# Token shift on two engines, softmax division after the value products, fused gate factors: one change to a two-layer encoder trunk

## The chip, the cores and the metric

The kernel runs on one core of one Trainium2 chip. The metric is the device time of one execution in microseconds, from several runs of the same kernel. Beside the runs there is one profiled execution, whose trace gives the start and length of each instruction on each engine: TensorE (PE, with its weight loads PEld), VectorE (DVE), ScalarE (ACT), GpSimd (POOL) and SyncE (SP), which issues most of the DMAs.

## What is computed

The input is 1024 frames of 1024 channels in float32. Layer 0 has an input projection whose columns feed two mixers: an RWKV-7 recurrence with 8 heads of 64, and a chunked band attention with 8 heads of 64. Layer 1 is a convolution module. Each layer ends with a squared-ReLU MLP. The change touches the two mixers of layer 0:

```python
# RWKV-7 group
p = p + (token_shift(p) - p) * mu                  # p[t-1] and p[t] mixed
r, k, v, xw, xa, xg = jnp.split(p, split_at, axis=-1)
w = -softplus(-(w0 + tanh(xw) @ w2)) - 0.5
decay = exp(-exp(w))
a = sigmoid(a0 + xa @ a2)
kk = normalise(k * k_k)                            # per head
k = k * (1 + (a - 1) * k_a)
# per step: S = S * decay + (S @ -kk) (kk * a)^T + v k^T ;  y = S @ r

# band attention, a chunk of 64 frames sees itself and 8 chunks before it
s = q @ k^T * HEAD_DIM ** -0.5 + bias
probs = jax.nn.softmax(s, axis=-1)
o = probs @ v
```

## The kernel before

Activations lie with channels on the 128 partitions and frames along the free dimension; the 1024 frames are done as two halves of 512. A dense matrix product (`gemm`, line 216) holds 128 output channels of 512 frames in one PSUM bank `d` and splits both operands into a rounded and a remaining part, so that each product is three matmuls, lines 263 to 265. The weights come by DMA (`wr`, line 203) and are split by ScalarE (`wh`, L207) and VectorE (`wl`, L208). The input projection's value columns are done with the operands the other way round and 256 columns at a time (L362 to L364); they are its last part in each half.

The recurrence (`rwkv`, line 375) takes blocks of 256 frames and pairs of heads, eight units in each half. Each unit has three stages. `prep` loads a tile `pt` of 257 frames from DRAM and mixes each frame with the one before (`mix`, L422 and L423, 14 times in a block of four units), makes decay and gate (L487 to L499, `ta` being the gate's tanh), the normalised key and the tiles `ar` and `bk` (L511 to L530), and their gram products (L549). The result goes out to DRAM and comes back in another layout (`msc`, `nb`). `stage2` inverts a triangular matrix on VectorE (L575 to L587), stores and loads the inverse through DRAM (`xsc`, `xdt`) and completes it with small matmuls (L612 and L622). `stage3` runs the chain over the chunks (L665, L670, L677, then L687 and L691) and the output norm (L700 to L718), and stores to `yd`.

The attention (`attention`, line 737) takes a head pair and 128 queries at a time, 32 groups in all. It makes scores in a PSUM bank `a`, of which there are two (L795, L797), adds the bias and finds the maximum (L799), takes the exponential with its sum (L806), divides (L807, L808), transposes the probabilities on TensorE (L817), copies them out (L818), multiplies by the values into another bank `a` (`ob`, L824), copies that out (`yo`, L827) and stores to `yd`.

The order of the instructions on each engine is set when the program is built. The code gives each piece a level: weight loads and evacuations come first, then the recurrence, then the attention, and the dense matmuls last, so that those fill what the mixers leave open on TensorE. On the chip each engine then takes its instructions strictly in that order. The dense work beside the first half's mixers is the input projection of both halves; beside the second half's mixers it is the output projection (`mixer_out`, which loads `yd` as `mh`) and the MLP of the first half. After the mixers there is only dense work and the convolution.

## Time and profile before

| | |
|---|---|
| runs, median (lowest to highest) | 2561.08 us (2558.75 to 2570.02) |
| profiled execution | 2570.09 us |
| its span, first to last instruction | 2568.2 us |
| granted TensorE clock, mean | 0.978 |
| TensorE busy | 2480.4 us, 97% |
| VectorE busy | 1848.3 us, 72% |
| ScalarE busy | 1143.9 us, 45% |
| instructions | 37380 |

Busy time is the union of an engine's instructions. A matmul's record is longer than the time it adds, since matmuls overlap. The granted clock is the share of full speed that TensorE had.

### The profile page before, as it was taken

To read this page: it belongs to the slowest core of one execution; us is meant where nothing else is said; L and a number is where in the kernel's file an instruction comes from. 1 tells how busy PE (TensorE), PEld (TensorE's weight loads), DVE (VectorE), ACT (ScalarE), POOL (GpSimd) and SP (SyncE) were. 2 spreads that over 40 slices of the span, in tenths; PEclk is the share of its full clock that TensorE was granted. 3 is DMA by queue.
4 is the path that set the end of the run, shared out by engine and by line. 5 is a ranking of instruction groups with operands and counts; after the bars stand their busy time and mean duration, and the time that the engine had idled before them with its cause. 6 is when DMAs were issued, how large, how long until landed. Compare 5 with 4: busy or idle time off the path is not lost.

```text
span 2568.2 us, 37380 instructions
## 1 busy us (share of the span) xinstructions
PE 2480.4 (97%) x12892; PEld 1971.0 (77%) x12892; DVE 1848.3 (72%) x3948; ACT 1143.9 (45%) x2224; POOL 111.6 (4%) x285
## 2 busy tenths in 40 slices
PE   8888999989999999999999999999999999999998
PEld 6667666757676767788888888888888888888887
DVE  5677788658788888546999974679999465544444
ACT  5345545555556655444343333533423355423324
POOL 1011001110000000000100000000000000000000
PEclk9898999989899999999999999999999999999999
DMA  8544444444333332236333333433333335333332
GB/s 266 157 141 137 115 121 119 140 130 119 95 104 107 102 101 81 77 107 197 95 93 100 96 99 99 140 115 95 95 99 99 99 91 156 95 95 98 99 97 68
DMA packets 476462, 291.24 MB, mean 113 GB/s; under 512 B 40416, under 2 KB 453472, under 8 KB 476272
## 3 DMA queue, kind: packets, MB, share of 16 engines
q1 hardware_dynamic: 466080, 258.11, 35.1%
q0 software_dynamic: 9152, 29.36, 3.3%
q8 instruction: 102, 1.67, 0.3%
q10 hardware_dynamic: 1040, 1.38, 0.2%
q14 instruction: 88, 0.72, 0.1%
HBM read 254.12 MB, written 37.77 MB: 114 GB/s over the span
## 4 chain that ended last, share of the span: by engine, by line
PE 82%; DVE 7%; DMA 6%; issue 3%; ACT 1%; SPq 0%; POOL 0%; ACTq 0%; DVEq 0%; POOLq 0%
PE d L264 23%; PE d L263 23%; PE d L265 23%; DMA nb<-msc 3%; DVE wl L208 1%; PE w L549 1%; PE a L824 1%; DVE pr L584 1%; DMA wr<-in_w_in_dram 1%; PE a L817 1%; PE c L665 1%; PE a L795 1%; DVE xi L587 1%; PE c L670 1%; DMA pt<-pd 1%
## 5 line engine op out<-in xcount | busy, mean ns | idle before, releaser
L207 ACT CAST wh<-wr 128x512 fp32r<-128x512 f32 x744 | 460.7, 621 | 988.9 <-PE d L264 897.2
L263 PE MATMUL d<-xh,wh 128*128 128x512 f32 x1872 | 748.4, 400 | 6.1 <-ACT xh L153 4.2
L264 PE MATMUL d<-xl,wh 128*128 128x512 f32 x1872 | 746.6, 399 | 0.8 <-DVE xl L154 0.4
L265 PE MATMUL d<-xh,wl 128*128 128x512 f32 x1872 | 746.3, 399 | 0.9 <-DVE wl L208 0.9
L208 DVE TENSOR_TENSOR wl<-wr,wh 128x512 fp32r<-128x512 f32 x744 | 501.9, 685 | 190.0 <-ACT wh L207 135.0
L263 PEld LDWEIGHTS d<-xh,wh 128*128 128x128 f32 x1872 | 356.9, 191 | 81.2 <-ACT xh L153 4.7
L264 PEld LDWEIGHTS d<-xl,wh 128*128 128x128 f32 x1872 | 356.5, 190 | 74.8 <-DVE xl L157 1.3
L265 PEld LDWEIGHTS d<-xh,wl 128*128 128x128 f32 x1872 | 356.5, 190 | 74.6 <-DVE wl L208 1.6
L263 PE MATMUL d<-mh,wh 128*128 128x512 f32 (+1 forms) x1040 | 405.9, 390 | 0.0
L264 PE MATMUL d<-ml,wh 128*128 128x512 f32 (+1 forms) x1040 | 405.2, 390 | 0.0
L265 PE MATMUL d<-mh,wl 128*128 128x512 f32 (+1 forms) x1040 | 404.9, 389 | 0.0
L947 DVE SCALAR_TENSOR_TENSOR cv<-u,dwt,cv 128x512 f32<-128x512 f32 x480 | 332.4, 746 | 0.7
L264 PEld LDWEIGHTS d<-ml,wh 128*128 128x128 f32 x1040 | 195.7, 188 | 38.9
L265 PEld LDWEIGHTS d<-mh,wl 128*128 128x128 f32 x1040 | 195.5, 188 | 39.1
L263 PEld LDWEIGHTS d<-mh,wh 128*128 128x128 f32 x1040 | 195.6, 188 | 38.4 <-issue 0.2
L846 DVE TENSOR_TENSOR x<-d,x 128x512 f32<-128x512 f32 (+1 forms) x146 | 97.6, 680 | 142.5 <-PE d L265 142.2
L888 DVE SCALAR_TENSOR_TENSOR t<-d,rstd 128x512 f32<-128x512 f32 x128 | 86.3, 686 | 101.2 <-PE d L265 98.1
L584 DVE TENSOR_TENSOR pr<-nb,xi 128x16 f32<-128x16 f32 (+15 forms) x256 | 101.0, 395 | 2.6
L894 DVE TENSOR_TENSOR ml<-t,mh 128x512 fp32r<-128x512 f32 x128 | 87.8, 688 | 13.5 <-ACT mh L892 10.9
L890 ACT ACTIVATE t<-t 128x512 f32<-128x512 f32 x128 | 80.1, 626 | 18.9 <-DVE t L888 18.4
L892 ACT ACTIVATE mh<-t 128x512 fp32r<-128x512 f32 x128 | 78.9, 616 | 0.0
L587 DVE TENSOR_REDUCE xi<-pr 128x8 f32<-128x16 f32 (+15 forms) x256 | 73.9, 289 | 2.4
(261 smaller groups left out, 2452.5 us busy)
## 6 DMA issues: line engine op xcount, KB each, us to landing
wr<-in_up_dram SPq DMA_DIRECT2D x256, 256.0 KB
wr<-in_dn_dram SPq DMA_DIRECT2D x256, 256.0 KB
wr<-in_w_in_dram SPq DMA_DIRECT2D x104, 256.0 KB
wr<-in_pw_dram SPq DMA_DIRECT2D x96, 256.0 KB
nb<-msc SPq DMA_DIRECT2D x16, 512.0 KB
wr<-in_w_out_dram SPq DMA_DIRECT2D x32, 256.0 KB
pd<-t POOLq DMA_DIRECT2D x28, 256.0 KB, 3.0
x<-xd SPq DMA_DIRECT2D x24, 256.0 KB
```

The costliest lines, as they stand in the source:

```text
L207: nc.scalar.copy(hi[:], raw[:])
L208: nc.vector.tensor_tensor(out=lo[:], in0=raw[:], in1=hi[:].bitcast(F32), op=ALU.subtract)
L263: nc.tensor.matmul(q[:, cols], hi, xh[:, cols], start=(k == 0), stop=False)
L264: nc.tensor.matmul(q[:, cols], hi, xl[:, cols], start=False, stop=False)
L265: nc.tensor.matmul(q[:, cols], lo, xh[:, cols], start=False, stop=(k == KT - 1))
L584: nc.vector.tensor_tensor(out=pr[:, :, :, 0:n], in0=pairs[:, r, :, 0:n].unsqueeze(2).to_broadcast([P, 2, 4, n]), in1=xi[:, :, 0:n].unsquee ...
L587: nc.vector.tensor_reduce(out=xi[:, :, n - 2 : n].rearrange("p j r -> p r j"), in_=pr[:, :, :, 0:n], op=ALU.add, axis=AX.X)
L846: nc.vector.tensor_tensor(out=xs[m][:, cols], in0=q[:, cols], in1=xs[m][:, cols], op=ALU.add)
L888: nc.vector.scalar_tensor_tensor(out=t[:], in0=q[:], scalar=0.0, in1=rstd[:], op0=ALU.max, op1=ALU.mult)
L890: nc.scalar.activation(sq[:], t[:], AF.Square)
L894: nc.vector.tensor_tensor(out=lo[:], in0=sq[:], in1=hi[:].bitcast(F32), op=ALU.subtract)
L947: nc.vector.scalar_tensor_tensor(out=c[:], in0=u[:, tap : tap + T], scalar=dw(tap), in1=c[:], op0=ALU.mult, op1=ALU.add)
```

## The change

The vector of coefficients gets 14 more columns, one minus `mu`. `mix` no longer takes a difference on VectorE: ScalarE scales the current frame by one minus `mu`, and VectorE adds the frame before times `mu`. The gate's tanh moves up beside the decay's. The gate's factor (tanh + 1) / 2 is no tile of its own: VectorE adds 1 and multiplies by the inverse decay in one instruction, and the factor 0.5 goes into the next one. In the attention the probabilities are not divided. The two heads' reciprocals of the sums go into a small tile `rr`; after the value products two more matmuls per group spread them over 64 partitions each (weights: one column of `rr`, repeated; moving operand: the identity), into the same PSUM bank. ScalarE copies them to `yo`, and VectorE multiplies the value products by them on the way out.

```diff
+    OMM = VOFF["dw"]
+    nc.vector.tensor_scalar(vec[:, OMM : OMM + 14], vec[:, 0:14], -1.0, 1.0, op0=ALU.mult, op1=ALU.add)
...
-            nc.vector.tensor_tensor(out=d[:], in0=t[:, 0:RT], in1=t[:, 1 : RT + 1], op=ALU.subtract)
-            nc.vector.scalar_tensor_tensor(out=dst, in0=d[:], scalar=v("mu", ct), in1=t[:, 1 : RT + 1],
+            nc.scalar.activation(d[:], t[:, 1 : RT + 1], AF.Copy, scale=vec[:, OMM + ct : OMM + ct + 1])
+            nc.vector.scalar_tensor_tensor(out=dst, in0=t[:, 0:RT], scalar=v("mu", ct), in1=d[:],
                                            op0=ALU.mult, op1=ALU.add)
...
             nc.scalar.activation(tw[:], wps, AF.Tanh, bias=half[:, hp : hp + 1], scale=0.5)
+            ta = e()
+            nc.scalar.activation(ta[:], aps, AF.Tanh, bias=half[:, 4 + hp : 5 + hp], scale=0.5)
             nc.scalar.activation(wx[:, :, 1 : C + 1], d3(tw[:]), AF.Exp, bias=kc[:, 3:4], scale=c1)
...
             yield
-            ta = e()
-            nc.scalar.activation(ta[:], aps, AF.Tanh, bias=half[:, 4 + hp : 5 + hp], scale=0.5)
             ksq = e()
...
-            nc.vector.tensor_scalar(aa[:], ta[:], 0.5, 0.5, op0=ALU.mult, op1=ALU.add)
-            nc.vector.tensor_tensor(out=aa[:], in0=aa[:], in1=dinv[:], op=ALU.mult)
+            nc.vector.scalar_tensor_tensor(out=aa[:], in0=ta[:], scalar=1.0, in1=dinv[:], op0=ALU.add, op1=ALU.mult)
...
-                nc.vector.tensor_tensor(out=bk[s, :, off : off + C], in0=d3(aa[s, :]), in1=d3(kkn[s, :]), op=ALU.mult)
+                nc.vector.scalar_tensor_tensor(out=bk[s, :, off : off + C], in0=d3(aa[s, :]), scalar=0.5,
+                                               in1=d3(kkn[s, :]), op0=ALU.mult, op1=ALU.mult)
...
+                rr = tiny.tile([P, 2], F32, tag="rr", name="rr", bufs=2)
...
-                    nc.vector.reciprocal(out=st[:, 4:5], in_=st[:, 3:4])
-                    nc.vector.tensor_scalar(pt[:, 0:w], pt[:, 0:w], st[:, 4:5], None, op0=ALU.mult)
+                    nc.vector.reciprocal(out=rr[:, hd : hd + 1], in_=st[:, 3:4])
...
+                for hd in range(2):
+                    nc.tensor.matmul(ob[hd * C : hd * C + C, P : 2 * P], rr[:, hd : hd + 1].to_broadcast([P, C]), ident,
+                                     start=True, stop=True)
                 yo = ap.tile([P, P], F32, tag="yo", name="yo", bufs=1)
-                nc.vector.tensor_copy(yo[:], ob[:, 0:P])
+                nc.scalar.copy(yo[:], ob[:, P : 2 * P])
+                nc.vector.tensor_tensor(out=yo[:], in0=ob[:, 0:P], in1=yo[:], op=ALU.mult)
```

Since the order of every engine is made anew when the program is built, much more moves than these lines. Behind the first added lines the line numbers are higher by about 2, and by 6 behind the attention.

TensorE at the end of the first half's recurrence, before. L362 to L364 are the last matmuls of the input projection, L670 to L691 the last chain, L700 the norm, L817 and L824 attention:

```order
L362 MATMUL d<-wh,xh 128x256
L363 MATMUL d<-wh,xl 128x256
L364 MATMUL d<-wl,xh 128x256
L670 MATMUL c<-zs_1654,xdt_1650 64x64 x2
L677 MATMUL c<-vs,bkt 64x64 x2
L817 MATMUL a<-cst,pt 128x128
L687 MATMUL c<-ar,vs 64x64 x8
L691 MATMUL c<-g,vs 64x64 x8
L817 MATMUL a<-cst,pt 128x128
L824 MATMUL a<-pT,vt 64x128
L700 MATMUL v<-y,cst 128x256
L824 MATMUL a<-pT,vt 64x128
```

The same place now; L689 and L693 are the chain's last products, L702 the norm, L364 to L366 the input projection:

```order
L689 MATMUL c<-ar,vs 64x64 x8
L693 MATMUL c<-g,vs 64x64 x8
L364 MATMUL d<-wh,xh 128x256
L365 MATMUL d<-wh,xl 128x256
L366 MATMUL d<-wl,xh 128x256
L364 MATMUL d<-wh,xh 128x256
L702 MATMUL v<-y,cst 128x256
L365 MATMUL d<-wh,xl 128x256
L366 MATMUL d<-wl,xh 128x256
L364 MATMUL d<-wh,xh 128x256
L365 MATMUL d<-wh,xl 128x256
L366 MATMUL d<-wl,xh 128x256
```

Before, no matmul of the projection was left when the last chain ended; now the chain ends with 174 of them still to come, and the norm's last matmul (L717, now L719) with 134.

SyncE's queue where the second half starts, before. `mh` are the loads of the mixers' outputs for the output projection, `wr` its weights, `pt` the first loads of the second half's recurrence:

```order
L871 DMA mh<-yd_130 128x512
L203 DMA wr<-in_w_out_dram 128x4x128 x2
L871 DMA mh<-yd_131 128x512
L416 DMA pt<-pd_105 128x257
L416 DMA pt<-pd_106 128x257
```

The same place now (`vt` are values for the attention of the second half):

```order
L877 DMA mh<-yd_130 128x512
L877 DMA mh<-yd_131 128x512
L877 DMA mh<-yd_132 128x512
L205 DMA wr<-in_w_out_dram 128x4x128 x4
L418 DMA pt<-pd_106 128x257
L418 DMA pt<-pd_107 128x257
L759 DMA vt<-vd 128x128 x4
```

The order of the loads is nearly the same, but on TensorE the first products of the second half (L483) now stand 20 matmuls ahead of the projection's end, where before they stood 62 full-size matmuls behind it.

## The prediction

> **What bounds the kernel now.** I read the page's busy shares first, then the windows by stage, then the waits of TensorE inside the stages that are not full.

> ```profile
> PE 2480.4 (97%) x12892; PEld 1971.0 (77%) x12892; DVE 1848.3 (72%) x3948; ACT 1143.9 (45%) x2224; POOL 111.6 (4%) x285
> ```

> ```profile
> 0.00:70.00 70.00, 59.75 (x278) 45.95 (x279) 33.94 (x58) 35.18 (x65) 10.53 (x38) 1.00 0.85 271
> 70.00:531.00 461.00, 425.05 (x2707) 317.91 (x2705) 352.39 (x999) 225.81 (x510) 51.36 (x128) 0.93 0.45 130
> 531.00:576.00 45.00, 32.67 (x171) 22.52 (x172) 22.94 (x66) 21.56 (x49) 6.04 (x20) 0.80 0.45 138
> 576.00:1060.00 484.00, 463.47 (x2978) 343.47 (x2978) 396.84 (x1158) 273.13 (x593) 17.79 (x57) 0.97 0.36 99
> 1060.00:2568.20 1508.20, 1499.46 (x6764) 1241.18 (x6763) 1042.15 (x1670) 588.23 (x1010) 25.83 (x42) 1.00 0.36 105
> ```

> The columns are window, length, then busy us and instructions of PE, PEld, DVE, ACT and POOL, then the granted clock, the DMA share and GB/s. TensorE is the bound, so removing work from VectorE pays only where TensorE waits. I call "loss" what a stage takes beyond its TensorE work at full clock: length minus busy time times clock. It is 10.3 us before 70, 461 - 425.05 x 0.93 = 65.7 in the first half's mixer stage, 45 - 32.67 x 0.80 = 18.9 in a short stage at 531, 484 - 463.47 x 0.97 = 34.4 in the second half's mixer stage, and 8.7 after 1060. The change touches only the mixer and attention, which are over at 1060. At most 119 us is there to be won, in three places.

> The short stage is the one to understand. Its TensorE rows in order of time (start, length, wait in brackets):

> ```profile
> 530.26 0.28 PE L362 MATMUL d<-wh,xh 128*128 128x256 f32 x1
> 530.38 0.28 PE L363 MATMUL d<-wh,xl 128*128 128x256 f32 x1
> 530.50 0.28 PE L364 MATMUL d<-wl,xh 128*128 128x256 f32 x1
> ...
> 532.71 0.34 PE L677 MATMUL c<-vs,bkt 128*64 128x64 f32 x4 [1.42 <-ACT vs L672]
> ...
> 566.54 0.39 PE L263 MATMUL d<-xh,wh 128*128 128x512 f32 x1
> 566.76 0.40 PE L264 MATMUL d<-xl,wh 128*128 128x512 f32 x1
> 567.00 0.40 PE L265 MATMUL d<-xh,wl 128*128 128x512 f32 x1
> 571.63 1.22 PE L263 MATMUL d<-xh,wh 128*128 128x512 f32 x2 [4.24 <-ACT xh L153]
> ...
> 575.72 0.80 PE L263 MATMUL d<-xh,wh 128*128 128x512 f32 x1 [0.37 <-DVE x L846]
> ```

> At 530.50 the input projection, the dense work that fills the gaps of the mixer, has run out. The last chain of the first half's recurrence and three groups of its attention are still to come. They run bare, one waiting for the other, until the output projection has its last input at 571.63 and flows at 575.72. Matmuls overlap, so the price of one is the step from start to start: 0.12 us for the half-size ones of the input projection's value part, 0.23 for the full-size ones.

> **The change part by part.** First what it takes from and gives to the engines:

> ```profile
> L422 DVE TENSOR_TENSOR e<-pt 128x256 f32<-128x256 f32 x56 | 23.4, 418 | 8.8 <-DMA pt<-pd 8.6
> L808 DVE TENSOR_SCALAR pt<-pt,st 128x640 f32<-128x640 f32 (+4 forms) x64 | 29.7, 466 | 0.6
> L518 DVE TENSOR_SCALAR e<-e 128x256 f32<-128x256 f32 x16 | 4.5, 280 | 0.0
> L514 DVE SCALAR_TENSOR_TENSOR ar<-e,dx 128x256 f32<-128x256 f32 x16 | 6.6, 415 | 0.0
> L501 ACT ACTIVATE e<-e,vec 128x256 f32<-128x256 f32 x16 | 8.0, 502 | 0.1
> L1000 ACT COPY u<-o 128x128 f32<-128x128 f32 x32 | 8.1, 265 | 8.9 <-PE o L992 5.8 <-DVE u L998 2.6
> L824 PE MATMUL a<-pT,vt 128*64 128x128 f32 x480 | 49.0, 297 | 0.1
> ```

> Off VectorE go the difference of the token shift (23.4 us), the division (29.7) and one step of the gate (4.5), 57.6 us in all, 7.5% of the 772 us it is busy from 70 to 1060. The fused forms cost nothing: a scalar_tensor_tensor with a constant takes 415 ns (L514), a tensor_tensor of the same length 418 (L422). ScalarE gains 56 scaled copies, nearest to L501's 502 ns, so 28.1 us, and 32 copies out of PSUM at 265 ns, 8.5 us. It is 45% busy, so neither is a bound; what hides them is its own idle time, and uncovered they would cost 36.6 us. The adjacent tanh pair changes little: the program has 64 table loads where it had 66. The multiply that takes the place of the copy at L827 reads the same tile and is counted equal. ScalarE now waits for the load of the shift where VectorE did (8.6 us in the L422 row); behind it stand the casts of the weights, and VectorE's part of that split waited behind the same load before, so I put this at 0.

> TensorE gains 64 matmuls that spread the reciprocals over the partitions (new line 829), with the shape of the value products, 64 columns of weights by 128. The profile has two records for each of those (480 for 240). The price of one is in the chain:

> ```profile
> 517.33 0.66 PE a L824 x10
> ```

> Ten records in 0.66 us, so 128 records take 8.4 us; at the group's mean of 49.0/480 = 102 ns they take 13.1. I take 8.4, since the new pairs also stand back to back, and since TensorE is the bound nothing hides them: +8.4. [...]

> Second, what moves. In the changed program the recurrence's last unit of the first half ends while 134 half-size matmuls of the input projection are still to come, and the attention of that half ends 58 earlier; before, none were left, and three groups of the attention came after them. So the bare stage at 531 goes: -18.9. What is late next is the start of the second half. Its first loads now stand on SP's queue behind the eight loads of the mixer's output and four weight tiles, and its first products stand on TensorE ahead of the last 20 projection matmuls, where everything dense queues behind them. The trace has the same start once, in the first half:

> ```profile
> PE v L612 <- DVE e L606: 14.3, 3, 6.3
> PE w L481 <- DVE xl L462: 5.8, 1, 5.8
> PE a L817 <- DVE pt L808: 3.8, 1, 3.8
> PE w L447 <- ACT e L445: 3.6, 2, 3.3
> PE v L603 <- DVE e L702: 2.9, 1, 2.9
> ```

> These are waits of TensorE between 70 and 531, in total, number and longest. The start (L481) waited 5.8 us, with its slow clock up to 8. With the 16 us of dense work that now lies in between (134 at 0.12 us) it may be nothing; I take the middle, +4.

> How a wait is priced with the clock hangs on these windows (two microseconds each, columns as above):

> ```profile
> 532.00:534.00 2.00, 0.87 (x11) 0.54 (x13) 1.62 (x7) 1.39 (x7) 0.71 (x1) 1.00 0.91 265
> 534.00:536.00 2.00, 2.00 (x33) 1.60 (x29) 0.26 (x1) 0.23 (x1) 0.00 (x0) 0.53 0.89 291
> 536.00:538.00 2.00, 2.00 (x7) 0.98 (x6) 0.18 (x1) 0.41 (x2) 0.00 (x0) 0.62 0.29 77
> ```

> A wait of 1.4 us was enough for some 3.5 us at half clock, so I count the whole of busy time times clock. [...]

> Two small effects cancel. The transposes (L817) no longer wait for the division, 0.47 us and a hand-over each, in five waits of TensorE at most 3.3 us. And the output tile now leaves PSUM in two steps, so that a score matmul that waits for the bank waits 0.27 us and a hand-over longer; behind it stand the dense matmuls.

> ```profile
> PE a L795 <- DVE yo L827: 5.9, 2, 3.5
> ```

> This wait of the second half came twice, so +0.8; if all 32 groups paid it, +12.8. I take the sum of both as 0.

> The sum: -18.9 + 4 + 8.4 = -6.5 us. The profiled execution took 2570.09 us (span 2568.2), 9 us above the median of the runs, 2561.08; it gives 2563.6, and on the median 2554.6. A measurement of this kernel can tell about 0.5% from no change, 12.8 us, so this is a small gain inside that.

> **The rivals.** *The lighter VectorE shortens the other waits too.* Of the 30.4 us in the five rows of waits above, 26.8 end with VectorE, and it becomes 7.5% lighter. A unit's inverse has this long from its last gram products:

> ```profile
> 98.33 1.74 PE L549 MATMUL w<-ar,bk 64*128 64x128 f32 x16
> ...
> 162.14 0.63 PE L612 MATMUL v<-e,g 32*32 32x32 f32 x16 [6.14 <-DVE e L606]
> ```

> 7.5% of these 62 us is 4.6, of which I count 4. The three waits at L612 would lose about 10, the others 4, so 14 more: 2540.6. For it: VectorE is 352/461 = 76% busy there and 82% in the second half. Against it: TensorE's order was tightened as well, so the time gained may be spent already. *The bare stage only changes its place:* the loads behind each other on SP cost the whole 18.9 at the start of the second half, and only the new matmuls remain: 2561.08 + 8.4 = 2569.5. For it: twelve of these tiles (the issues between 531 and 576, with their size) stand ahead of its loads.

> ```profile
> mh<-yd SPq DMA_DIRECT2D x8, 256.0 KB
> wr<-in_w_out_dram SPq DMA_DIRECT2D x5, 256.0 KB
> ```

> Against it: the last result they wait for is ready 16 us of dense work earlier. *Slower: the cover of the inverse was cut, the inverse was not.* Between the last gram product (L549) and the first product on the inverse (L612), over the eight units of the first half, the program now has 1078 full-size dense matmuls where it had 1192, 247 half-size where it had 374, and 1058 small ones where it had 897. At 0.23, 0.12 and 0.132 us (the pace of L824) that is 26.2 + 15.2 - 21.3 = 20 us less. The inverse passes through DRAM twice, which no lighter VectorE shortens. It decides if those units have no slack; three of eight had none before (the L612 row). With all 20 us turned into waiting and 2 of slow clock it is 2576.6.

> **How the numbers follow.** The forecast gets 0.48: its own range is 2550.6 to 2563.3 (the start at 0 to 8, the new matmuls at 8.4 to 13.1). The lighter VectorE gets 0.20, the stage that changes place 0.17, the cut cover 0.15. Faster by over 0.5% (below 2548.3) are 0.19 of the second case and 0.09 of the first, where order alone moves the waits further: 0.28. Slower (above 2573.9) are 0.13 of the cut cover, 0.02 of the moved stage and 0.01 of the forecast: 0.16. That leaves 0.56. The range goes from 2537 (the lighter VectorE without a wait at the start) to 2576 (just short of the full cut), some 0.2 outside.

> **What would show it.** Right: no stretch of 20 us below 0.8 clock between the last half-size projection matmul and the first full-size ones of the output projection; 128 records of line 829 at some 66 ns; TensorE's loss between 70 and the end of the first recurrence near 66. Wrong: waits at the inverse's first product (new line 614) well above 14.3 us in sum, a wait of over 8 us for a load at the start of the second half, or waits of the scores for the output tile in most groups.

## The result: 1.2% slower, and the profile after

| | before | changed |
|---|---|---|
| runs, median (lowest to highest) | 2559.95 us (2558.75 to 2570.02) | 2591.25 us (2585.2 to 2600.96) |
| ratio, 95% interval | | 1.0117 (1.0073 to 1.0161) |
| profiled execution | 2570.09 us | 2586.63 us |
| its span | 2568.2 us | 2584.9 us |
| TensorE busy | 2480.4 us | 2511.3 us |
| VectorE busy | 1848.3 us | 1811.3 us |

The median before is over one run more than the 2561.08 us ahead of the forecast. Medians and ratios, here and in the experiments, leave out slow runs; there was one, of e7 (3020.09 us at a granted clock of 0.748).

The forecast was 2554.6 us and no change; the kernel became 31 us slower. First the busy shares of the changed kernel, then its windows by stage (columns as in the prediction):

```profile
PE 2511.3 (97%) x13020; PEld 1976.4 (76%) x13020; DVE 1811.3 (70%) x3813; ACT 1169.7 (45%) x2310; POOL 109.9 (4%) x285
```

```profile
0.00:70.00 70.00, 59.99 (x274) 45.59 (x275) 33.79 (x58) 35.49 (x65) 10.53 (x38) 1.00 0.84 269
70.00:531.00 461.00, 428.44 (x2734) 312.39 (x2733) 338.27 (x966) 241.01 (x565) 52.28 (x135) 0.93 0.45 130
531.00:576.00 45.00, 43.82 (x292) 37.98 (x292) 28.70 (x72) 29.42 (x61) 5.71 (x15) 1.00 0.69 205
576.00:1060.00 484.00, 462.89 (x3016) 341.54 (x3015) 365.79 (x1059) 280.33 (x620) 20.58 (x65) 0.98 0.34 93
1060.00:2584.90 1524.90, 1516.19 (x6711) 1238.95 (x6709) 1044.79 (x1659) 583.42 (x1001) 20.82 (x32) 1.00 0.35 104
```

The bare stage at 531 us is gone, as forecast: TensorE is busy for 43.82 of 45 us at full clock, where it was 32.67 at 0.80. But the last window is 1524.9 us long where it was 1508.2, with TensorE full and at clock 1.00 in both. That is the part of the program which the change was said not to touch. Its loss, as length minus busy time times clock, is 8.7 us before and after (1508.20 - 1499.46, 1524.90 - 1516.19): the added time counts as TensorE's busy time, not as waiting. The groups of its dense matmuls tell where it went. Before, the three matmuls of each product on the mixed input and other normed activations (`xh`, `xl`), and the first on the MLP's middle tiles (`mh`); the columns after the count are busy us in total and mean ns of one record:

```profile
L263 PE MATMUL d<-xh,wh 128*128 128x512 f32 x1872 | 748.4, 400 | 6.1 <-ACT xh L153 4.2
L264 PE MATMUL d<-xl,wh 128*128 128x512 f32 x1872 | 746.6, 399 | 0.8 <-DVE xl L154 0.4
L265 PE MATMUL d<-xh,wl 128*128 128x512 f32 x1872 | 746.3, 399 | 0.9 <-DVE wl L208 0.9
...
L263 PE MATMUL d<-mh,wh 128*128 128x512 f32 (+1 forms) x1040 | 405.9, 390 | 0.0
```

The same groups of the changed kernel:

```profile
L265 PE MATMUL d<-xh,wh 128*128 128x512 f32 x1872 | 757.4, 405 | 3.0 <-ACT wh L209 2.7
L266 PE MATMUL d<-xl,wh 128*128 128x512 f32 x1872 | 753.4, 403 | 0.0
L267 PE MATMUL d<-xh,wl 128*128 128x512 f32 x1872 | 751.1, 401 | 0.9 <-DVE wl L210 0.9
...
L265 PE MATMUL d<-mh,wh 128*128 128x512 f32 (+1 forms) x1040 | 406.1, 391 | 0.0
```

As many instructions of the same shape cost 9.0, 6.8 and 4.8 us more, 20.6 together, when the moving operand is `xh` or `xl`, and 0.2 when it is `mh`. In order of time the pace can be read off directly. Seven starts in the dense stretch before, of which the first and the last are shown:

```profile
1930.31 0.39 PE L263 MATMUL d<-xh,wh 128*128 128x512 f32 x1
...
1931.67 0.39 PE L263 MATMUL d<-xh,wh 128*128 128x512 f32 x1
```

And seven starts at nearly the same place of the changed kernel:

```profile
1930.20 0.40 PE L266 MATMUL d<-xl,wh 128*128 128x512 f32 x1
...
1931.60 0.40 PE L266 MATMUL d<-xl,wh 128*128 128x512 f32 x1
```

Six steps take 1.36 us before and 1.40 after, 227 and 233 ns, without a wait between them. Over all such steps from 1100 to 2520 us the mean goes from 226.8 to 232.3 ns on `xh` and `xl` and from 226.7 to 226.8 on `mh` and `ml`. From the 3000th to the 9000th dense matmul in the trace it is 1378.1 us before and 1397.6 after. So nearly two thirds of the 31 us are lost where the instructions are the same in number, shape and clock.

What differs there is an address. The new tile `rr` takes two slots of 32 bytes on every partition, and every pool opened behind it moves up by 64 bytes. The tiles `wh`, `wl`, `mh` and `ml` and four `xh` of the part after the mixers lie behind it, eight `xh` and eight `xl` ahead of it. First byte on each partition in the program as built, and its remainder by 256:

```
                  before          changed
xh, first 8       38400 (0)       38400 (0)
wh                92160 (0)       92224 (64)
mh               124928 (0)      124992 (64)
xh, last 4       165888 (0)      165952 (64)
```

Before, all of these agree by 256. In the changed kernel the weights have moved against the first eight `xh` and `xl`; `mh` and the last four `xh` and `xl` have moved with them. The matmuls of the trace, taken in order with the tiles of the program as built, show both: from 1100 to 2520 us a step between two matmuls on the first eight is 233.3 ns, on the last four 228.6, on `mh` and `ml` 226.8.

### The profile page after: what moved, and what is told of

It reads as the page before. It is cut to its first block, busy times and chain, and to the rows that moved or that the text cites. A ratio compares the mean times of both kernels' runs of the same rounds, so it can differ in the third digit from the quotient of the medians.

```text
span 2584.9 us, 37658 instructions
## 1 busy us (share of the span) xinstructions
PE 2511.3 (97%) x13020; PEld 1976.4 (76%) x13020; DVE 1811.3 (70%) x3813; ACT 1169.7 (45%) x2310; POOL 109.9 (4%) x285
## 4 chain that ended last, share of the span: by engine, by line
PE 65%; DVE 2%; DMA 1%; issue 0%; SPq 0%; ACT 0%; ACTq 0%; DVEq 0%
PE d L265 21%; PE d L266 21%; PE d L267 21%; DMA nb<-msc 1%; DVE pr L586 0%; PE o L998 0%; PE a L826 0%; PE w L551 0%; DVE xi L589 0%; DVE wl L210 0%; PE a L819 0%; PE c L679 0%; PE c L667 0%; PE a L798 0%; DMA xdt<-xsc 0%
## 5 line engine op out<-in xcount | busy, mean ns | idle before, releaser
L265 PE MATMUL d<-xh,wh 128*128 128x512 f32 x1872 | 757.4, 405 | 3.0 <-ACT wh L209 2.7
L265 PEld LDWEIGHTS d<-xh,wh 128*128 128x128 f32 x1872 | 355.5, 190 | 86.2 <-ACT wh L209 3.4
L265 PE MATMUL d<-mh,wh 128*128 128x512 f32 (+1 forms) x1040 | 406.1, 391 | 0.0
L265 PEld LDWEIGHTS d<-mh,wh 128*128 128x128 f32 x1040 | 195.9, 188 | 39.3 <-issue 0.6
L896 ACT ACTIVATE t<-t 128x512 f32<-128x512 f32 x128 | 80.0, 625 | 24.2 <-DVE t L894 23.7
## 6 DMA issues: line engine op xcount, KB each, us to landing
wr<-in_up_dram SPq DMA_DIRECT2D x256, 256.0 KB
wr<-in_dn_dram SPq DMA_DIRECT2D x256, 256.0 KB
wr<-in_w_in_dram SPq DMA_DIRECT2D x104, 256.0 KB
wr<-in_pw_dram SPq DMA_DIRECT2D x96, 256.0 KB
wr<-in_w_out_dram SPq DMA_DIRECT2D x32, 256.0 KB
pd<-t POOLq DMA_DIRECT2D x28, 256.0 KB, 2.7
x<-xd SPq DMA_DIRECT2D x24, 256.0 KB
```

The costliest lines, as they stand in the source:

```text
L265: nc.tensor.matmul(q[:, cols], hi, xh[:, cols], start=(k == 0), stop=False)
L896: nc.scalar.activation(sq[:], t[:], AF.Square)
```

## The experiments

Theory: the loss is the 64 bytes between weights and moving operand. Rival: the loss comes from the changed work in the mixers. Each run was compared with the kernel before on the same chip. Medians are in us.

| run | median | ratio to before (95%) | order of instructions |
|---|---|---|---|
| e1 the change, no new tile | 2561.85 | 1.0011 (0.9995 to 1.0027) | of the changed kernel |
| e2 before, unused 64 bytes | 2578.01 | 1.0076 (1.0051 to 1.0101) | of before |
| e3 before, weights 64 against the rest | 2583.6 | 1.0085 (1.0055 to 1.0116) | of before |
| e4 before, tiles behind the weights 64 up | 2568.49 | 1.0042 (1.0025 to 1.0059) | of before |
| e10 before, weights and all behind 128 up | 2571.43 | 1.0058 (1.0038 to 1.0077) | of before |
| e11 the same, 32 up | 2579.59 | 1.0103 (1.0075 to 1.013) | of before |
| e12 the same, 256 up | 2556.58 | 1.0011 (0.9994 to 1.0028) | of before |
| e5 mix split alone | 2567.25 | 1.0057 (1.0036 to 1.0078) | its own |
| e6 division moved alone | 2551.52 | 0.9992 (0.9977 to 1.0007) | its own |
| e7 gate and tanh alone | 2564.73 | 1.0045 (1.0024 to 1.0065) | its own |
| e8 mix, gate and tanh | 2564.5 | 1.0036 (1.0022 to 1.005) | its own |
| e9 as e8, division on ScalarE | 2557.6 | 1.0009 (0.9997 to 1.0021) | its own |

**The address alone.** The first run is the changed kernel with the reciprocals left where they were; every engine keeps the changed kernel's order, as the two traces show (13020 records on TensorE, the same shapes in the same order):

```diff
-                rr = tiny.tile([P, 2], F32, tag="rr", name="rr", bufs=2)
+                rr = []
...
-                    nc.vector.reciprocal(out=rr[:, hd : hd + 1], in_=st[:, 3:4])
+                    nc.vector.reciprocal(out=st[:, 4:5], in_=st[:, 3:4])
+                    rr.append(st[:, 4:5])
...
-                    nc.tensor.matmul(ob[hd * C : hd * C + C, P : 2 * P], rr[:, hd : hd + 1].to_broadcast([P, C]), ident,
+                    nc.tensor.matmul(ob[hd * C : hd * C + C, P : 2 * P], rr[hd].to_broadcast([P, C]), ident,
```

> The changed kernel with the two reciprocals kept in the statistics tile st instead of a new tile rr: same instructions in the same order on every engine, but all pools behind that small pool lie 64 bytes lower, where they lay before the change. Placement theory (the 64 bytes cost the dense matmuls about 5 ns in each of those that read xh and xl): the dense steps of the up and in projections fall from 0.233 to 0.227 us, the stretch from 1060 us to the end loses about 20 us, and the time is about 2570 us, ratio to the kernel before near 1.004. Rival (the slow dense stretch comes from the new order or from the extra work, not from addresses): no change, 2591 us, ratio 1.012.

The second is the kernel before with an unused tile of 64 bytes:

```diff
+    tiny.tile([P, 16], F32, tag="pad", name="pad")
```

> The kernel before with one unused tile of 64 bytes in the small pool: same instructions in the same order on every engine, all later pools 64 bytes higher. Placement theory: the dense stretch gets some 20 us longer, about 2580 us, ratio 1.008. Rival (order or extra work): no change, ratio 1.000.

Measured: without the tile the change is 1.0011 times the kernel before; with 64 unused bytes the kernel before is 1.0076 times itself. The pace of TensorE in one window of 200 us tells the two apart at a glance (window, length, TensorE's busy us and instructions, clock, DMA share, GB/s). Before, the changed kernel, e1 and e2:

```profile
1900.00:2100.00 200.00, 200.00 (x887) 1.00 0.34 98
```

```profile
1900.00:2100.00 200.00, 200.00 (x872) 1.00 0.33 95
```

```profile
1900.00:2100.00 200.00, 200.00 (x887) 1.00 0.32 94
```

```profile
1900.00:2100.00 200.00, 200.00 (x872) 1.00 0.33 95
```

872 against 887 matmuls in the same 200 us is 1.7%, whichever kernel's order it is. From the 3000th to the 9000th dense matmul e1 takes 1378.2 us and e2 1397.6, the figures of before and of the changed kernel. The spans of the changed kernel and of e1, whose work and order are the same, differ by 2584.9 - 2560.7 = 24.2 us. The rival falls as the cause of the slowdown: the order and the work stay and the loss goes (e1), or they stay as before and the loss comes (e2). e1 came out some 8 us faster than its expectation, which counted on the dense stretch alone. By ratio, e2's 0.76% and e1's 0.11% make 0.87%, inside the interval of the change as a whole (0.73 to 1.61%); what else of its 1.17% may be real, these runs can't tell.

**Which distance counts.** The third run moves only the weights by 64 bytes and sets what lies behind them 128 up, both in the part after the mixers alone. The pool `padq` is opened ahead of the weights' pool there, `padp` behind it:

```diff
+        padq.tile([P, 16], F32, tag="padq", name="padq")
+        padp.tile([P, 16], F32, tag="pad", name="pad")
```

> The kernel before, in its second phase (the dense part from about 1090 us) only the split weights wh and wl 64 bytes higher, everything else as before modulo 128. If the place of the weights relative to the moving operand counts: both kinds of dense steps, of xh and of mh, get slower, by 20 to 40 us in all (2580 to 2600). If only the moving operand's own place counts: no change, 2560. If the weights' own place alone counts: xh and mh slower alike.

The fourth has the second of these tiles alone, so that the weights stay and what lies behind them moves by 64 bytes.

> The kernel before, in its second phase only the tiles behind the weights (mh, ml and four of the xh and xl tiles) 64 bytes higher, the weights where they were. If the relative place counts: steps of mh and ml slower than 0.227 us, those of xh mostly as before, some 10 to 20 us in all (2570 to 2580). If the weights' own place counts: no change, 2560.

Measured, mean steps from 1100 to 2520 us: in e3 232.0 ns on `xh` and `xl` and 228.7 on `mh` and `ml`; in e4, where only the last four `xh` and `xl` and the middle tiles have moved, 228.4 and 228.8. So `mh`, which lost nothing when it moved together with the weights, loses when one of the two moves, and a part of the `xh` tiles moved gives a part of the loss. In these runs the loss goes with the distance between the two, not with the address of either. The paces of e3 and e4:

```profile
1900.00:2100.00 200.00, 200.00 (x868) 1.00 0.33 95
```

```profile
1900.00:2100.00 200.00, 200.00 (x878) 1.00 0.33 97
```

I took the modulus for 128 bytes. The next run puts one unused tile of 128 bytes ahead of the weights, and two more make it 256 and 32:

```diff
+        padq.tile([P, 32], F32, tag="padq", name="padq")
```

> The kernel before with an unused tile of 128 bytes a partition ahead of the weights in the projections' part: the weights and all behind them go up by 128 bytes, twice the shift that cost 20 us; the front tiles of the mixed input stay. Theory (what counts is the distance of weights and moving operand modulo 128 bytes): no loss, 2553 to 2563 us, steps of 226.8 ns for both kinds of operand. Rival (any displacement between the two costs, or the addresses' higher bits do, or the added tile's waits): 15 us or more slower, steps of 230 ns or more.

> The kernel before with an unused tile of 256 bytes a partition ahead of the weights in the projections' part. The 128-byte shift left steps of 231.7 ns for the tiles of the mixed input that stay, so the modulus of 128 bytes has fallen. Theory (weights and moving operand have to agree modulo 256 bytes): steps of 226.8 ns for both kinds of operand, 9000 of them in the same time as before, 2551 to 2561 us. Rival (they have to agree modulo 512 bytes, the length of a weight row): steps of 231 to 232 ns for the mixed input, 227 for the middle ones, and 15 to 20 us slower.

> The same with an unused tile of 32 bytes a partition. Theory (any disagreement costs the same): steps of 231 to 232 ns for the mixed input, 15 to 20 us slower. Rival (the shift counts from 64 bytes on, half of it or nothing below): steps of at most 229.5 ns, at most 10 us slower.

The paces at 128, 256 and 32 bytes:

```profile
1900.00:2100.00 200.00, 200.00 (x876) 1.00 0.33 95
```

```profile
1900.00:2100.00 200.00, 200.00 (x887) 1.00 0.33 95
```

```profile
1900.00:2100.00 200.00, 200.00 (x871) 1.00 0.33 96
```

At 128 bytes the pace stays low (mean steps 231.7 ns on `xh` and `xl`, 226.8 on `mh` and `ml`), so 128 was wrong. At 256 the full pace is back (226.8 ns on `xh` and `xl`, 226.7 on `mh` and `ml`), and the whole kernel is again 1.0011 times before, which cannot be told from no change. 32 bytes cost as much as 64 in the steps (232.1 ns on `xh` and `xl`, against 232.3 in the changed kernel), though the whole kernel lost 24 us, more than the 15 to 20 expected. Of the shifts by 32, 64, 128 and 256 bytes that were run, only the last cost nothing that could be measured.

**What the parts of the change are worth without the address.** The rest of the runs add no tile. The division alone (the reciprocals in `st`, the 64 products, the copy and the multiply as in the change):

```diff
-                    nc.vector.tensor_scalar(pt[:, 0:w], pt[:, 0:w], st[:, 4:5], None, op0=ALU.mult)
+                    rr.append(st[:, 4:5])
...
+                for hd in range(2):
+                    nc.tensor.matmul(ob[hd * C : hd * C + C, P : 2 * P], rr[hd].to_broadcast([P, C]), ident,
+                                     start=True, stop=True)
...
```

> The kernel before with the softmax division alone moved behind the value products (the 64 small products with the identity, the copy on ScalarE and the product on VectorE for each output tile; the reciprocals stay in the fifth column of the tile that holds them, so no address changes). Theory (the loss of the change as a whole lies in where the weights stand, not in the mixer): VectorE loses 128 multiplications of 29.7 us, TensorE gains 64 pairs of some 8 us, of which part lies under waits: within 8 us of the kernel before, between 2550 and 2566 us. Rival (the extra products cost, and something else in the change pays for them, so that the whole with its addresses kept came out even): 8 to 13 us slower, 2566 to 2571 us, with waits of TensorE for the reciprocals above 13 us.

(There are 64 of these multiplications, as the prediction's row of L808 has it, not 128.) The theory held: 2551.52 us, with TensorE waiting 0.3 us in all for the reciprocals.

Mix, gate and tanh as in the change, the division left:

```diff
-            nc.vector.tensor_tensor(out=d[:], in0=t[:, 0:RT], in1=t[:, 1 : RT + 1], op=ALU.subtract)
+            nc.scalar.activation(d[:], t[:, 1 : RT + 1], AF.Copy, scale=vec[:, OMM + ct : OMM + ct + 1])
...
-            nc.vector.tensor_scalar(aa[:], ta[:], 0.5, 0.5, op0=ALU.mult, op1=ALU.add)
-            nc.vector.tensor_tensor(out=aa[:], in0=aa[:], in1=dinv[:], op=ALU.mult)
+            nc.vector.scalar_tensor_tensor(out=aa[:], in0=ta[:], scalar=1.0, in1=dinv[:], op0=ALU.add, op1=ALU.mult)
...
```

> The kernel before with the mix split over ScalarE and VectorE and with the gate and tanh edits, the division left where it was; no tile is added. Theory (placement is the loss, the mixer parts are worth what was forecast for them): VectorE loses 28 us in the first half and TensorE gets nothing new; the stretch before 1060 us gains the forecast's terms without the extra products, so -5 to -15 us against the kernel before if the bare stretch at 531 us closes, 2542 to 2552 us; 0 if it does not. Rival (mixer edits only move waits, as the whole with its addresses kept did): within 4 us, 2553 to 2561 us. In both the dense stretch after 1060 us runs at 227 ns a step.

The same with the division on ScalarE:

```diff
-                    nc.vector.tensor_scalar(pt[:, 0:w], pt[:, 0:w], st[:, 4:5], None, op0=ALU.mult)
+                    nc.scalar.activation(pt[:, 0:w], pt[:, 0:w], AF.Copy, scale=st[:, 4:5])
```

> As the run with the mix split and the gate edits, and the division done by ScalarE ahead of the transposes instead of by VectorE; TensorE gets no instruction more. ScalarE takes 128 multiplications of about 0.23 to 0.35 us, some 30 to 45 us over the first half, and VectorE is lighter by 57 us as in the full change. Theory that VectorE's load in the scores matters: a gain of 8 us or more over the kernel before and more than the run without it, 2540 to 2549 us. Rival (VectorE's share there is hidden; ScalarE, which makes the exponentials, is the one waited for): not faster than the run without it, with more waits of the transposes for ScalarE.

Then the first and the second half of e8's diff, each by itself.

> The kernel before with the token-shift mix alone split over ScalarE and VectorE. The run with the mix and the gate edits was 9 us slower than the kernel before, though VectorE did 28 us less in it. Theory (the mix is the one that costs: ScalarE now stands ahead of VectorE in it, so the mixed input, for which the projections wait, comes later by ScalarE's queue): 5 to 12 us slower, 2560 to 2567 us, with waits of TensorE for the mixed input's parts in the first 70 us and at the start of the second half longer than before by together 5 us or more. Rival (the gate and tanh edit costs): within 3 us of the kernel before.

> The kernel before with the fused gate factors and the tanh pair alone. Theory (the mix costs): within 3 us of the kernel before, 2552 to 2558 us. Rival (the gate and tanh edit costs, since the second tanh now stands ahead of the sigmoid's and decay's steps, on which the recurrence waits): 5 to 12 us slower, 2560 to 2567 us, and the bare stretch at 531 us stays at a clock below 0.9.

Both guesses on e8 missed: it is 9 us slower than before, not even or faster, though VectorE has 28 us less to do; the bare stage did not close. The guesses on the cause missed too: I had expected one of mix and gate to carry it, and each alone costs as much as both, 0.57% and 0.45%. What grows in these kernels is a wait of TensorE that the mixer edits do not touch, that of the transposes for the division (0 to 1060 us; total, times, longest). Before, e5, e7 and e8:

```profile
PE a L817 <- DVE pt L808: 7.1, 5, 3.8
```

```profile
PE a L819 <- DVE pt L810: 15.1, 6, 5.8
```

```profile
PE a L817 <- DVE pt L808: 10.5, 5, 4.7
```

```profile
PE a L819 <- DVE pt L810: 8.7, 6, 3.9
```

Each edit makes the order of every engine anew, and in these orders TensorE reaches the transposes earlier than VectorE the division. With the division behind the value products this wait does not exist. That division edit alone costs nothing measurable in spite of its 64 matmuls, and the whole change without the tile (e1) stands at 0.11%, below either mixer edit alone. The effects do not add.

That this wait is the reason is not shown, and the stages speak against it as the whole reason. In size it fits best in e5 (15.1 - 7.1 = 8.0 us of 0.57%, 14.6 us), less in e7 (3.4 of 11.5) and e8 (1.6 of 9.2). But by length minus busy time times clock, e5 loses most in the second half's mixer stage:

```profile
576.00:1060.00 484.00, 465.17 (x2941) 344.44 (x2940) 385.46 (x1124) 278.61 (x614) 17.49 (x57) 0.95 0.35 96
```

This is 484 - 465.17 x 0.95 = 42.1 us, where seven profiles of before's order have 22.6 to 34.4, and the wait for the division makes only 5.3 us in that window (1.1 before). e7 loses 37.1 us there, with 3.5 us of that wait. e8 does not lose there (18.9) but from 70 to 531 us: 70.2, against 56.4 to 67.2. With one profile each, why e5, e7 and e8 are slower stays open.

With the division on ScalarE the kernel is back at 1.0009, but the wait is not gone, it has changed its engine:

```profile
PE a L819 <- ACT pt L810: 7.9, 4, 3.2
```

Neither guess on e9 held: it does not gain 8 us, but it is faster than e8, at 2557.6 against 2564.5 us. ScalarE took 64 multiplications of 693 ns, 44.0 us in all; the 0.23 to 0.35 us for one in the expectation was the author's estimate and is shown by no run.

No version here beats the kernel before by more than its interval; e6, at 0.9992, comes nearest.

## Why the prediction was wrong, point by point

**The step that failed** is this sentence: "The change touches only the mixer and attention, which are over at 1060." It counted the dense stretch at its old length. The instructions there are the same, but the tile `rr` in the diff moved the weights, and the stretch lost some 20 of the 31 us. The diff showed the tile, and I priced what is written into it and not where it lies. None of the rivals held this either: all of them stayed in the mixers. Of the 24.2 us between the changed kernel and e1, 4.7 had been lost by the 3000th dense matmul, at 1145.9 us. Before 1100 us, too, the steps between neighbouring matmuls on `xh` and `xl` are longer (233.6 ns against 230.0 in e1); how much of the 4.7 us that makes was not split further. The prediction's signs for being right or wrong all came out on the right side, as the terms below show: they watched the mixers alone and could not show this step.

**The mixer's sum** can be tested on e1, which has the change without the address: forecast -6.5 us, measured +2.8 (-1.3 to +6.9, from the interval). So the gain that was forecast did not come, and the sum was some 9 us off. Term by term:

*The bare stage, forecast -18.9.* Right. What ran bare there now has the last projection matmuls beside it. In six other profiles of before's order the stage's loss lies between 16.2 and 18.3, against 1.2 in the changed kernel and in e1. One reading of its rows was too short, though the sum does not hang on it: it was not the wait of 1.42 us alone that went before the low clock (0.53 from 534 to 536 us). From 531 to 534 us TensorE was busy for only 1.16 us, at a clock of 1.00. What of this brought the clock down, and how long a wait has to be for it, was not shown.

*The start of the second half, forecast +4 (0 to 8).* The place was wrong. At 567 us the changed kernel waits 0.56 us for a score, and no load is waited for. But the second half's mixer stage probably became worse. The windows of e2, in before's order:

```profile
70.00:531.00 461.00, 429.06 (x2689) 319.58 (x2689) 350.35 (x991) 223.73 (x504) 51.29 (x128) 0.92 0.45 129
531.00:576.00 45.00, 33.60 (x190) 23.99 (x189) 23.66 (x71) 22.13 (x50) 5.46 (x16) 0.83 0.46 139
576.00:1060.00 484.00, 464.77 (x3016) 343.11 (x3015) 401.23 (x1169) 276.27 (x602) 18.59 (x61) 0.99 0.37 101
```

The windows of e1, in the changed kernel's order:

```profile
70.00:531.00 461.00, 426.55 (x2751) 312.64 (x2749) 337.30 (x966) 241.42 (x566) 52.27 (x135) 0.93 0.45 131
531.00:576.00 45.00, 43.84 (x284) 37.53 (x283) 30.89 (x77) 30.67 (x62) 5.72 (x15) 1.00 0.65 200
576.00:1060.00 484.00, 461.24 (x3019) 340.83 (x3018) 364.09 (x1054) 278.48 (x618) 20.23 (x65) 0.98 0.34 93
```

By length minus busy time times clock the last of these loses 32.0 us, and 23.9 in e2. The profile of before on which the prediction stood showed 34.4 there; of seven profiles of that order it is the highest, and the median is 23.7. The changed kernel has 30.4. Both lie inside the range of the seven, and the clock's two decimals leave some 2 us open, so that about 8 us came back in the second half is likely and not shown. The one profile hid how little there was to lose there.

*The waits that came in its place.* TensorE's longest waits of the changed kernel from 0 to 1060 us:

```profile
PE w L538 <- DVE e L535: 8.6, 5, 6.4
PE w L449 <- ACT e L447: 6.9, 3, 3.4
PE v L624 <- DVE e L714: 5.5, 3, 2.5
PE v L614 <- DVE e L608: 5.4, 3, 4.9
PE v L638 <- DVE e L720: 4.6, 3, 1.9
PE w L483 <- DVE xl L464: 4.6, 1, 4.6
...
PE a L829 <- DVE rr L810: 3.0, 2, 2.5
```

The inverse's first product (L614, before L612) waits 5.4 us where it was 14.3, so the cut cover, the slower rival, is not what happened. No wait of the scores for the output tile is left (5.9 before), and none of the transposes for the division (3.8 in the first half). In their place have grown the wait for the bonus term's product (L538, 3.3 us before) and those of the inverse's second product and of the transposes for steps of the output norm (L624, 3.0 us before, and L638, none before). The waits at the spread of the norms (L449) are about as long as before, 10.0 us over both its banks against 9.1. The rival of the lighter VectorE gave 14 us for shorter waits; they changed places instead, although VectorE is 37 us less busy.

*The 64 matmuls, forecast +8.4 (8.4 to 13.1).* Not contradicted. Four of them in a row:

```profile
311.07 0.49 PE L829 MATMUL a<-cst,rr 128*64 128x128 f32 x4 [0.50 <-DVE rr L810]
```

One record alone is 0.27 us, so a further one adds (0.49 - 0.27) / 3 = 73 ns, where 66 was forecast; 128 of them are 9.4 us. Counted from start to start, with the longer step to the next kind of matmul, which the value products paid before, all 128 take 15.3 us in e1. The term is known to some 9 to 15 us. But e6 has them all and is not slower than before. Its window at 531 us shows a part of what pays for them:

```profile
531.00:576.00 45.00, 41.62 (x226) 32.96 (x225) 33.30 (x79) 25.87 (x52) 4.32 (x20) 0.92 0.61 175
```

The bare stage loses 45 - 41.62 x 0.92 = 6.7 us there, against 16.2 to 18.9 in before's order, 14.0 in e8 (36.45 us busy at 0.85), 10.4 in e5 and 11.5 in e7. Every new order closes a part of it, that of the division's move the most.

The sum of the terms as the runs show them, -15 to -18 for the bare stage, likely +8 in the second half, +9 to +15 for the matmuls and about nothing in the first half (loss 64.3 in e1, 56.4 to 67.2 in the seven of before's order), is -1 to +8, around the +2.8 of e1. The loss from 70 to 531 us, "near 66" in the forecast, is 62.6.

## What to carry over

The new tile of 8 bytes a partition, in two buffers, moved every tile of the pools opened behind it by 64 bytes here, and the dense stretch took some 20 us more. Before costing a change, list the start addresses of the operands of the costliest instructions before and after, and compare the distances between weights and moving operands; when a stretch that the diff doesn't touch changes its pace at a full clock, look there first. Where a small tile is needed, put it into a spare column of one that exists, or behind the hot pools. And one profile's loss in a stage is not the kernel's: here the same stage had 22.6 to 34.4 us in seven profiles of one order, more than the effect that was forecast from it.
